# A list scheduler that plays the program through on another machine model: a two-layer diffusion block on one core

## Chip, cores and metric

The kernel runs on one core of one Trainium2 chip. The metric is device time in microseconds (us) of one execution; lower is better.

## What is computed

The reference is a two-layer block over 512 latent tokens and 256 context tokens of width 1024, batch 1, all in float32. Each layer normalises its input and shifts and scales it by vectors that come from a condition (adaptive modulation: six vectors of 1024 for each layer and each of the two streams). The first layer mixes tokens by pooling windows and a neighbourhood attention with context, the second by a recurrence over time (an RWKV layer) with heads of 64; each is followed by a squared-ReLU MLP. Two further layers with a gated MLP and a second mixer end the program. Cut to the parts that the change touches most:

```python
def rms_norm(x, g):
    y = xf * lax.rsqrt(jnp.mean(xf * xf, axis=-1, keepdims=True) + RMS_EPS)
    return (y * g.astype(jnp.float32)).astype(x.dtype)

def modulate(h, shift, scale):
    return h * (1 + scale) + shift

def neighbourhood_attention(q, k, v, k_ctx, v_ctx, rpb):
    ...
        s_lat = jnp.where(col_ok[:, None, :], s_lat + bias, NEG_INF)
        s_ctx = jnp.einsum('bqhd,bchd->bhqc', q_row, k_ctx).astype(jnp.float32) * scale
        s = jnp.concatenate([s_lat.reshape(B, NA_HEADS, GRID_W, kr * GRID_W), s_ctx], axis=-1)
        p = jax.nn.softmax(s, axis=-1).astype(v.dtype)
```

## The kernel before

The program is one launch of some 69,000 instructions. Matrices are multiplied in a three-term split: each float32 operand is held as a high and a low part (a cast on ScalarE writes `wh` from the loaded block `wr`, a subtraction on VectorE or GpSimd writes `wl`; activations have tiles `a` for both parts), and TensorE adds high*high, low*high and high*low. Weights are loaded on SyncE's one DMA queue in blocks of 512 KB through a ring of `wr` buffers.

The stages stand in this order in time. 0 to about 100 us: modulation for the first sub-layer, norms, keys and values of a memory. About 100 to 411 us: the first layer's mixer, that is its projections (`pj` banks), 24 units of attention (`ps` banks; VectorE adds the mask `nab` to the scores with a running maximum, ScalarE takes the exponent, VectorE splits and scales) and the pooled part (`pu`, `pw`, `t`), whose projection weights are `ev_u`. 411 to about 560 us: the tail of the pooled part, eight splits of the mixer's result (`a_874` to `a_881`), the output projection (`ev_o`), residual and norm. 600 to 1080 us: the first MLP. Then the recurrent layer's features to 1400 us, its recurrence (`wkv`) to 2120 us, its output and MLP to 2600 us, and the two last layers.

One job stands beside these. Each modulation vector block (128 outputs for one layer) needs a 512 KB block of `adaT` and two dot products on VectorE, one for each stream: `junk<-ada,c_rows` and `junk<-ada,cc_rows`, 128x1024 each, followed by a short read of the accumulator into `mod`. They will be called dots; there are 96 blocks, 192 dots. Blocks come through a ring of two buffers `ada` (the first 16 in part through `wr`), so the load of block m+2 waits on SyncE for the dots of block m. `First.ada_g` (line 552) writes the loop:

```python
for m in ms:
    w = c.ring(self.silp, [P, D], "ada", 2)
    nc.sync.dma_start(w, c.A["adaT"][i, m])
    yield from self.ada_dot(i, mod, m, [w], self.junk())
```

Blocks 0 to 15 of layer 0 are needed at the start; blocks 16 to 39 stand in the text beside the mixer; blocks 40 to 47 and the 48 of layer 1 (`ada` in `second_half`, line 1077, and `ada1`, line 1184) stand beside the output projection and the MLP that follows, and layer 1's are first used after that MLP, at about 1080 us.

What sets the order. The kernel's own planner (`Clock.weave`) decides in which order the Python text issues the instructions. The framework's `TileContext` then schedules this list: on a model of the machine, an engine that comes free takes, of its instructions whose operands the model has ready, the one that stands first in the list. So work that stands far behind may be put ahead into time that the model sees as free. Each engine then executes its instructions strictly in the order that results, and SyncE issues its DMAs in order, too.

## Time and profile before

| | before |
|---|---|
| time, median of 3 runs | 4526.43 us (4525.61 to 4526.72) |
| the profiled execution | 4529.56 us, of which 4527.8 us are the span from first to last instruction |
| TensorE (PE) busy | 4146.5 us, 92% of the span |
| VectorE (DVE) busy | 2583.0 us, 57% |
| ScalarE (ACT) busy | 1747.0 us, 39% |
| GpSimd (POOL) busy | 1150.1 us, 25% |
| mean granted TensorE clock | 0.945 of full speed |

All instructions are recorded by one helper, so they share the line L176; tiles and stretches of time tell them apart. The stages have different limits: TensorE is busy all the time in the MLPs, and in the mixers, the recurrence and the stretch around the output projection it has gaps. The profiled execution took 3.1 us more than the median of the runs.

### The profile page before, as it was taken

The page shows a single profiled execution, that of the slowest core. Times are in us where ns is not written, and L with a number is a line of the kernel's source. Part 1 is how long each engine was busy: PE and PEld are TensorE (multiplying, and loading weights), DVE is VectorE, ACT ScalarE, POOL GpSimd, SP SyncE. Part 2 cuts the span into 40 slices and gives each one's busy share as a digit, 9 for nine tenths or more (in the row PEclk, how much of TensorE's full clock was granted, in tenths as well). Part 3 has the DMA queues.
Part 4 walks back from the last instruction along what each step waited for, and adds up shares of the span by engine and source line. Part 5 has one row for each costly group of instructions (what it writes and reads, how often), then busy time and mean ns, then how long its engine had stood idle before and what let it go on. Part 6 is the DMA issues. An engine that isn't in the chain of part 4 may idle for free. (4 is left out here: it accounts for less than half of the span.)

```text
span 4527.8 us, 69045 instructions
## 1 busy us (share of the span) xinstructions
PE 4146.5 (92%) x27872; PEld 3436.0 (76%) x27872; DVE 2583.0 (57%) x4105; ACT 1747.0 (39%) x3265; POOL 1150.1 (25%) x1122
## 2 busy tenths in 40 slices
PE   5897899997897988887999999988999999979998
PEld 4786688886685777766888788876888888857887
DVE  8998844345934666677644543486433433584333
ACT  4454422223534556544522432225322322334222
POOL 4223300003514344453200211163201201353111
PEclk8898999999898899988999999998999999979999
DMA  6444421212233111112432322220332323211332
GB/s 220 148 134 134 148 75 62 65 63 96 84 122 102 42 46 52 47 40 63 137 107 94 98 95 97 93 76 18 103 98 94 97 96 96 93 38 62 97 98 84
DMA packets 193889, 408.80 MB, mean 90 GB/s; under 512 B 46496, under 2 KB 87456, under 8 KB 193568
## 3 DMA queue, kind: packets, MB, share of 16 engines
q1 hardware_dynamic: 193568, 404.37, 27.8%
q8 instruction: 219, 3.59, 0.3%
q14 instruction: 102, 0.84, 0.1%
HBM read 386.47 MB, written 17.83 MB: 89 GB/s over the span
## 5 line engine op out<-in xcount | busy, mean ns | idle before, releaser
L176 PE MATMUL pj<-a,wh 128*128 128x512 f32 (+1 forms) x5328 | 1420.2, 356 | 73.7 <-DVE a L176 32.2
L176 PE MATMUL ps<-a,wh 128*128 128x512 f32 x4192 | 1293.4, 390 | 12.0 <-DVE a L176 6.4
L176 ACT CAST wh<-wr 128x1024 fp32r<-128x1024 f32 (+3 forms) x548 | 565.2, 1031 | 1643.9 <-PE ps L176 952.6
L176 PEld LDWEIGHTS pj<-a,wh 128*128 128x128 f32 x5328 | 951.6, 195 | 221.8 <-issue 43.7
L176 PE MATMUL pj<-a,wl 128*128 128x512 f32 (+1 forms) x2664 | 939.2, 353 | 26.5 <-DVE wl L176 20.5
L176 PEld LDWEIGHTS ps<-a,wh 128*128 128x128 f32 x4192 | 786.5, 188 | 176.9 <-DVE a L176 7.5
L176 PE MATMUL ps<-a,wl 128*128 128x512 f32 x2096 | 815.5, 389 | 0.0
L176 DVE TENSOR_TENSOR wl<-wr,wh 128x1024 fp32r<-128x1024 f32 (+3 forms) x490 | 599.1, 1223 | 301.9 <-ACT wh L176 269.7
L176 PEld LDWEIGHTS pj<-a,wl 128*128 128x128 f32 x2664 | 517.9, 195 | 102.2 <-DVE wl L176 26.7
L176 PEld LDWEIGHTS ps<-a,wl 128*128 128x128 f32 x2096 | 393.8, 188 | 81.8
L176 POOL TENSOR_TENSOR t<-t,a 128x512 f32<-128x512 f32 x94 | 159.6, 1699 | 1113.4 <-ACT t L176 1113.4
L176 POOL TENSOR_TENSOR a<-a,t 128x512 f32<-128x512 f32 (+1 forms) x109 | 142.1, 1306 | 1023.0 <-ACT t L176 1021.6
L176 PE MATMUL ps<-a,a 128*128 128x256 f32 (+4 forms) x859 | 195.7, 383 | 35.4 <-ACT a L176 15.1
L176 ACT CAST f<-ps 128x512 f16<-128x512 f32 x312 | 178.0, 587 | 119.9 <-PE ps L176 117.9
L176 DVE SCALAR_TENSOR_TENSOR ytm<-ps,ytm 128x512 f32<-128x512 f32 x96 | 66.4, 692 | 264.9 <-PE ps L176 264.9
L176 DVE TENSOR_TENSOR t<-t,ps 128x512 f32<-128x512 f32 x87 | 59.8, 688 | 275.2 <-PE ps L176 270.6
L176 DVE TENSOR_TENSOR a<-a,pj 128x512 f32<-128x512 f32 (+1 forms) x176 | 101.2, 578 | 166.9 <-PE pj L176 166.9
L176 PEld LDWEIGHTS <-bd 128*128 128x128 f16 x3264 | 139.8, 102 | 72.3 <-issue 24.7
L176 PEld LDWEIGHTS ps<-a,a 128*128 128x128 f32 (+1 forms) x859 | 136.2, 212 | 73.0 <-ACT a L176 24.3
L176 POOL TENSOR_TENSOR wl<-wr,wh 128x1024 fp32r<-128x1024 f32 x58 | 150.8, 2605 | 148.1 <-ACT wh L176 126.2
L176 DVE TENSOR_TENSOR t<-ps,a 128x512 f32<-128x512 f32 x86 | 59.2, 691 | 220.5 <-PE ps L176 220.5
L176 DVE SCALAR_TENSOR_TENSOR a<-a,c_cvw,a 128x511 f32<-128x511 f32 (+15 forms) x180 | 177.7, 1007 | 2.3
(301 smaller groups left out, 5557.7 us busy)
## 6 DMA issues: line engine op xcount, KB each, us to landing
wr<-in_f1w SPq DMA_DIRECT2D x120, 512.0 KB, 3.5
wr<-in_f2w SPq DMA_DIRECT2D x120, 512.0 KB, 3.5
ada<-in_adaT SPq DMA_DIRECT2D x88, 512.0 KB, 3.6
wr<-in_m0w SPq DMA_DIRECT2D x76, 512.0 KB, 3.6
wr<-in_m1w SPq DMA_DIRECT2D x76, 512.0 KB, 3.6
wr<-in_ev_o SPq DMA_DIRECT2D x16, 512.0 KB, 3.9
wr<-in_w_o SPq DMA_DIRECT2D x16, 512.0 KB, 3.5
k<-d_k SPq DMA_DIRECT2D x48, 128.0 KB, 2.2
```

Source lines behind the costliest of these rows:

```text
L176: return real(*a, **k)
```

## The change

The scheduler is asked to play the program on its second machine model, a timeline simulator, in place of its default model. Nothing else in the kernel's text differs.

```diff
-    with tile.TileContext(nc) as tc:
+    with tile.TileContext(nc, schedule_with_timeline_sim=True) as tc:
         build(tc, A)
```

The instructions are the same ones (the same counts on every engine); their order on each engine differs in many places. Counted over the order of both kernels, with the dots that stand on VectorE ahead of one and the same instruction:

```
instruction on VectorE            its start before   dots ahead: before   after
first mask step near 148 us                  147.7                   55      67
a_385, near 200 us                           200.0                   76     100
sum4_495, near 250 us                        250.3                   93     130
rc_582, near 300 us                          300.5                  112     149
a_679, near 346 us                           346.0                  129     183
a_705, near 358 us                           358.5                  135     192
t_842 (pooled part), near 411 us             411.3                  151     192
ms_1036 (first norm), near 492 us            492.2                  180     192
```

**VectorE in the attention, shortly before 346 us.** `a_649` to `a_665` are splits of attention scores that TensorE multiplies next (`a<-ps,a`, 128x512); `junk_*` are the dots. Before:

```order
L176 ISA junk_1324_6052,mod_1220_5402<-ada_1323_6050,cc_rows_6_108,c_adab_72 128x1024
L176 ISA mod_1220_5402 128x1
L176 ISA junk_1326_6081,mod_1218_5400<-ada_1325_6079,c_rows_5_105,c_adab_72 128x1024
L176 ISA mod_1218_5400 128x1
L176 TENSOR_TENSOR a_654_2934<-ps_652_2928,a_653_2933 128x512
L176 TENSOR_TENSOR a_658_2943<-ps_656_2937,a_657_2942 128x512
L176 SCALAR_TENSOR_TENSOR t_715_3191<-pw_714_3189,pu_697_3146 128x512
L176 TENSOR_TENSOR a_662_2952<-ps_660_2946,a_661_2951 128x512
L176 TENSOR_TENSOR a_665_2974<-ps_663_2968,a_664_2973 128x512
L176 TENSOR_TENSOR a_668_2982<-ps_666_2976,a_667_2981 128x512
```

After, at the same splits:

```order
L176 ISA junk_1532_7350,mod_1218_5400<-ada_1531_7348,c_rows_5_105,c_adab_72 128x1024
L176 ISA mod_1218_5400 128x1
L176 ISA junk_1532_7350,mod_1220_5402<-ada_1531_7348,cc_rows_6_108,c_adab_72 128x1024
L176 ISA mod_1220_5402 128x1
L176 TENSOR_TENSOR a_654_2934<-ps_652_2928,a_653_2933 128x512
L176 TENSOR_TENSOR a_658_2943<-ps_656_2937,a_657_2942 128x512
L176 ISA junk_1545_7425,mod_1218_5400<-ada_1544_7423,c_rows_5_105,c_adab_72 128x1024
L176 ISA mod_1218_5400 128x1
L176 ISA junk_1545_7425,mod_1220_5402<-ada_1544_7423,cc_rows_6_108,c_adab_72 128x1024
L176 ISA mod_1220_5402 128x1
L176 TENSOR_TENSOR a_662_2952<-ps_660_2946,a_661_2951 128x512
L176 TENSOR_TENSOR a_665_2974<-ps_663_2968,a_664_2973 128x512
```

Before, two dots stand ahead of these splits and one step of the pooled part (`t_715`) among them; after, four dots (two whole blocks) stand ahead of and among them, and the blocks are later ones (`ada_1531` and `ada_1544` against `ada_1323` and `ada_1325`).

**VectorE at the splits ahead of the output projection, 427 to 438 us.** `a_878` to `a_881` and `a_874` on are the splits of the mixer's result, `wl_992` a split of an `ev_o` block. Before:

```order
L176 TENSOR_TENSOR a_878_3901<-a_200_708,a_870_3893 128x512
L176 ISA junk_1464_6914,mod_1218_5400<-ada_1463_6912,c_rows_5_105,c_adab_72 128x1024
L176 ISA mod_1218_5400 128x1
L176 TENSOR_TENSOR a_879_3902<-a_201_709,a_871_3894 128x512
L176 ISA junk_1464_6914,mod_1220_5402<-ada_1463_6912,cc_rows_6_108,c_adab_72 128x1024
L176 ISA mod_1220_5402 128x1
L176 TENSOR_TENSOR a_880_3903<-a_202_710,a_872_3895 128x512
L176 TENSOR_TENSOR wl_992_4071<-wr_990_4068,wh_991_4070 128x1024
L176 TENSOR_TENSOR a_881_3904<-a_203_711,a_873_3896 128x512
L176 ISA junk_1473_6981,mod_1218_5400<-ada_1472_6979,c_rows_5_105,c_adab_72 128x1024
L176 ISA mod_1218_5400 128x1
```

After:

```order
L176 TENSOR_TENSOR a_878_3901<-a_200_708,a_870_3893 128x512
L176 TENSOR_TENSOR a_879_3902<-a_201_709,a_871_3894 128x512
L176 TENSOR_TENSOR wl_992_4071<-wr_990_4068,wh_991_4070 128x1024
L176 TENSOR_TENSOR a_880_3903<-a_202_710,a_872_3895 128x512
L176 TENSOR_TENSOR a_881_3904<-a_203_711,a_873_3896 128x512
L176 TENSOR_TENSOR a_874_3897<-a_196_704,a_866_3889 128x512
L176 TENSOR_TENSOR a_875_3898<-a_197_705,a_867_3890 128x512
L176 TENSOR_TENSOR a_876_3899<-a_198_706,a_868_3891 128x512
L176 TENSOR_TENSOR a_877_3900<-a_199_707,a_869_3892 128x512
```

All dots are gone from between the splits: none is left at this point.

**TensorE in the attention, at 341 to 350 us.** `ps_*` are attention products; `pj_719` and `pj_789` are the projections of the pooled part (`ev_u`), of the first and the second of its four groups. Before:

```order
L176 MATMUL ps_688_3096<-a_584_2619,a_637_2871 128x512
L176 MATMUL ps_688_3096<-a_585_2620,a_637_2871 128x512
L176 MATMUL ps_688_3096<-a_584_2619,a_638_2872 128x512
L176 MATMUL ps_690_3102<-a_583_2618,a_637_2871 128x256 x2
L176 MATMUL ps_690_3102<-a_583_2618,a_638_2872 128x256
L176 MATMUL ps_690_3102<-a_583_2618,a_637_2871 128x256 x2
L176 MATMUL ps_690_3102<-a_583_2618,a_638_2872 128x256
L176 MATMUL pj_719_3198<-a_151_563,wl_641_2880 128x512
L176 MATMUL pj_719_3198<-a_152_564,wh_640_2879 128x512
L176 MATMUL pj_719_3198<-a_160_572,wh_640_2879 128x512
```

After, at a place of the attention that comes earlier (`ps_663` was at about 340 us):

```order
L176 MATMUL ps_663_2968<-c_ident_61,a_618_2775 128x128 x4
L176 MATMUL ps_646_2895<-a_653_2933,a_405_1694 128x256
L176 MATMUL pj_789_3510<-a_170_582,wh_717_3194 128x256
L176 MATMUL pj_789_3510<-a_166_578,wl_718_3195 128x256
L176 MATMUL pj_789_3510<-a_167_579,wh_717_3194 128x256
L176 MATMUL pj_789_3510<-a_171_583,wh_717_3194 128x256
L176 MATMUL pj_789_3510<-a_167_579,wl_718_3195 128x256
L176 MATMUL pj_789_3510<-a_167_579,wh_717_3194 128x256
L176 MATMUL pj_789_3510<-a_171_583,wh_717_3194 128x256
L176 MATMUL pj_789_3510<-a_167_579,wl_718_3195 128x256
```

Before, most of the first group's projection (`pj_719`) stands behind the products of the unit with `ps_690`; after, the second group's (`pj_789`) already stands among products ahead of them. Over the whole order, 91 rows `pj<-a,wh` and `pj<-a,wl` that stood behind `ps_678` (the input of `a_679`) stand ahead of it now; with the durations that they had in the trace of before these are 16.8 us of TensorE.

On SyncE, in the same stretch, the last `adaT` load (`ada_7707`) stood 50 loads behind the first load of `ev_o` (`wr_4062`) and now stands five ahead of it. At the start, two mask loads (`nab`, 458 KB each) now stand ahead of `adaT` loads that were ahead of them. From 600 to 1040 us every engine has the order it had. In the later stages instructions change places with their neighbours; the work ahead of one and the same instruction differs by mostly under 5 us in either direction (at a few places of the features and the last mixers by up to 20 us) and comes back to zero within each stage.

## Rows read from the trace of the kernel before

**Rows 1.** The page's head and part 1: span, busy time of each engine.

```profile
span 4527.8 us, 69045 instructions
...
PE 4146.5 (92%) x27872; PEld 3436.0 (76%) x27872; DVE 2583.0 (57%) x4105; ACT 1747.0 (39%) x3265; POOL 1150.1 (25%) x1122
```

**Rows 2.** Busy time by stretch (us), TensorE's clock, share of DMA, GB/s.

```profile
core 0: us, PE busy (x) PEld busy (x) DVE busy (x) ACT busy (x) POOL busy (x), PEclk, DMA share, GB/s
0.00:100.00 100.00, 55.52 (x203) 36.08 (x204) 85.71 (x122) 46.96 (x105) 43.50 (x35) 0.88 0.65 227
100.00:346.00 246.00, 217.70 (x1331) 192.10 (x1330) 225.61 (x478) 122.04 (x302) 59.48 (x28) 0.90 0.42 141
346.00:411.00 65.00, 57.26 (x342) 50.06 (x341) 56.62 (x144) 40.55 (x100) 20.14 (x20) 0.92 0.32 105
411.00:427.00 16.00, 4.15 (x8) 1.86 (x7) 13.31 (x29) 4.82 (x10) 8.77 (x9) 0.58 0.46 144
427.00:444.00 17.00, 7.50 (x18) 5.32 (x18) 17.00 (x22) 7.38 (x17) 10.93 (x8) 0.50 0.45 144
444.00:560.00 116.00, 101.94 (x504) 81.06 (x503) 96.00 (x126) 49.69 (x84) 42.47 (x30) 0.93 0.53 170
...
600.00:1000.00 400.00, 400.00 (x2292) 352.66 (x2291) 162.20 (x239) 96.06 (x144) 0.00 (x0) 1.00 0.20 63
```

**Rows 3.** The same stretches, the dots alone (instructions that read `ada`).

```profile
100.00:346.00 246.00, 142.94 (x95) 0.90 0.42 141
346.00:411.00 65.00, 31.84 (x23) 0.92 0.32 105
411.00:427.00 16.00, 7.17 (x6) 0.58 0.46 144
427.00:444.00 17.00, 9.05 (x6) 0.50 0.45 144
444.00:560.00 116.00, 45.05 (x30) 0.93 0.53 170
```

**Rows 4.** VectorE's groups by form, 100 to 411 us: the dots.

```profile
L176 DVE CUSTOM_DVE_ANT_0 junk<-ada,cc_rows,c_adab 128x1024 bf16<-128x1024 f32 x58 | 92.2, 1590 | 0.6
L176 DVE CUSTOM_DVE_ANT_0 junk<-ada,c_rows,c_adab 128x1024 bf16<-128x1024 f32 x59 | 83.0, 1408 | 10.0 <-DMA ada<-in_adaT 9.5
```

**Rows 5.** What VectorE waited for, 100 to 346 us: total us, times, longest.

```profile
DVE junk L176 <- DMA ada<-in_adaT: 7.8, 8, 1.8
DVE a L176 <- ACT a L176: 4.8, 6, 1.4
```

**Rows 6.** VectorE in order of time, 427 to 438 us: start, duration.

```profile
427.66 1.75 DVE L176 CUSTOM_DVE_ANT_0 junk<-ada,c_rows,c_adab 128x1024 bf16<-128x1024 f32 x1
...
429.34 1.20 DVE L176 TENSOR_TENSOR a<-a,a 128x512 fp32r<-128x512 f32 x1
430.47 1.27 DVE L176 CUSTOM_DVE_ANT_0 junk<-ada,cc_rows,c_adab 128x1024 bf16<-128x1024 f32 x1
...
434.47 1.21 DVE L176 TENSOR_TENSOR a<-a,a 128x512 fp32r<-128x512 f32 x1
435.60 1.74 DVE L176 CUSTOM_DVE_ANT_0 junk<-ada,c_rows,c_adab 128x1024 bf16<-128x1024 f32 x1
...
437.27 1.20 DVE L176 TENSOR_TENSOR a<-a,a 128x512 fp32r<-128x512 f32 x1
```

**Rows 7.** TensorE in order of time, ahead of the output projection; idle before in brackets.

```profile
432.18 1.22 PE L176 MATMUL pj<-a,wh 128*128 128x512 f32 x2 [4.19 <-ACT a L176]
438.53 0.79 PE L176 MATMUL pj<-a,wh 128*128 128x512 f32 x1 [5.13 <-DVE a L176]
```

**Rows 8.** Busy time by stretch: features, recurrence, one late mixer; columns as in 2.

```profile
1040.00:1400.00 360.00, 308.40 (x1566) 251.83 (x1564) 207.39 (x302) 149.44 (x263) 134.32 (x154) 0.92 0.31 101
1400.00:2120.00 720.00, 614.33 (x10410) 501.02 (x10410) 488.48 (x942) 401.41 (x919) 315.05 (x452) 0.89 0.17 48
2960.00:3130.00 170.00, 142.56 (x662) 110.64 (x660) 134.31 (x255) 60.67 (x157) 82.35 (x68) 0.86 0.14 46
```

## The prediction

> **What bounds the kernel now.** The page's first part comes first: TensorE is busy 92% of the span, VectorE 57% [rows 1]. That average hides that the stages have different limits, so the next view is busy time by stretch [rows 2]. In the first MLP (600 to 1000 us) TensorE is busy 400.00 of 400 us and VectorE 162.20: nothing there waits for VectorE, and a delay that comes into this stretch goes through it unreduced. In the first mixer it is the other way round. From 100 to 346 us VectorE is busy 225.61 of 246 us (92%), TensorE 217.70 (88%); from 346 to 411 us the two have 56.62 and 57.26 of 65 us. The third view, the dots alone in the same stretches [rows 3], shows what fills VectorE: 142.94 us of the 225.61 are dots, of which none feeds the attention. The attention's own steps need 82.7 us there. Behind the mixer, 444 to 560 us, VectorE is busy 96.00 of 116 us, 45.05 of it dots.
>
> So the stretch from 100 to 411 us is set by VectorE and TensorE together, with little slack in either, and whatever is put into VectorE's queue there in front of the attention's steps makes these later.
>
> **The change, part by part.** The instructions are the same; only places change. I price each move with durations of the trace.
>
> *Dots moved ahead of the attention.* By the counts in the section on the change, 129 dots stand ahead of `a_679` (346 us) before, 183 after: 54 more. Later, at 358 us, all 192 are ahead. The dots that now run from 346 us on take 31.84 + 7.17 + 9.05 + 45.05 = 93.11 us in 65 entries [rows 3] (63 dots, two of them across a boundary), 1.43 us each; those of 100 to 411 us take 1.41 and 1.59 us, by the two forms [rows 4]. 54 x 1.43 = 77.3 us of VectorE are put in front of `a_679`.
>
> How much of this hides? VectorE's idle time up to there is 246 - 225.61 = 20.4 us [rows 2]. If the added dots squeeze out all of it, `a_679` is 77.3 - 20.4 = 56.9 us late; if none, 77.3 us. Of the idle time 7.8 us are dots that waited for their own load [rows 5]: with more dots in a row this part doesn't shrink. I take the other 12.6 us as squeezed out: 64.7 us late. The rest of the idle time is steps that waited for ScalarE and TensorE [rows 5], which will be ahead of VectorE then.
>
> *From there to the end of the mixer.* VectorE has less left than before: of 56.62 us in 346 to 411 us the dots' 31.84 go, and the last 9 dots (192 - 183) come, 12.9 us: 37.7 us. TensorE has 57.26 us less the 16.8 us of pooled projections that its order now puts ahead of that point: 40.5 us. The larger, TensorE, sets this part: 40.5 us back to back, or 46.0 us at the 88% that it reached before. Against the 65 us of before this gives back 24.5 or 19.0 us. The mixer's end is late by 56.9 - 24.5 = 32.4 us at the least, 77.3 - 19.0 = 58.3 us at the most while the 16.8 us are really done in the holes that the late attention leaves, and 64.7 - 19.0 = 45.7 us as I take it. If TensorE can't do the projections ahead (their weights stand behind `adaT` loads on SyncE, which wait for dots), it is 77.3 us.
>
> *Dots that are gone behind the mixer.* At 427 to 438 us three dots of 1.75, 1.27 and 1.74 us stand in turn between splits of the mixer's result [rows 6]; the last of the splits shown ends at 438.47, and TensorE starts its next product at 438.53 after 5.13 us idle [rows 7]. Without them the split comes some 4.5 us sooner (their durations less the overlap of some 0.1 us): -4.5. In 411 to 427 us 7.17 us of dots stand in a chain of short steps while TensorE does only 4.15 us of work in 16 [rows 2, 3]; some stood in waits, so I take half, -3.6, between 0 and -7.2. From 444 to 560 us TensorE is idle 14.1 us in all and 45.05 us of dots leave; I take -3, between 0 and -14.1. Sum -11, from -4.5 to -25.8.
>
> *The start.* Two mask loads of 458 KB each go ahead of `adaT` loads. At the 227 GB/s of that stretch [rows 2] they take 4.0 us, and VectorE, at 85.71 of 100 us, needs those dots. I take half, +2, between 0 and +8 (the same again for a store that now stands among them).
>
> *The later stages.* From 600 to 1040 us the order is the same: 0, TensorE being full. In the features, the recurrence and the late mixers TensorE has 51.6, 105.7 and 27.4 us of idle time in the stretches shown [rows 8], but moves there are small and of both signs, and no engine has more work ahead of it at a stage's end: 0, within 15 either way.
>
> *Sum*, against the profiled execution (4527.8 us of span and 1.8 around it, 4529.6): 45.7 - 11 + 2 + 0 = +36.7, so 4566.3. That execution was 3.1 us above the median of the runs; taken off, **4563 us**.
>
> A rule of the Trainium skill gives another result. Its page "Perfetto Trace Analysis" (section "Identifying the Most-Contended Engine") names the engine with the highest occupancy as the one that matters; for TensorE it goes by the weight loads' busy share. Over the whole kernel that is TensorE by either measure (92%, or 76% of weight loads, against 57%), so moving VectorE's work would be free: the first rival below. The page's next section adds that the most contended engine can change from regime to regime and that such regimes may be interleaved; by that sentence work should leave this mixer for the MLP, the opposite of what the change does.
>
> **The rivals.**
>
> *The dots hide.* TensorE is the kernel's bound, its order has changed as well, and the late attention is filled with projections; what is late at 411 us is caught up by 560, where 61.3 us of dots have left VectorE [rows 3]. For it: TensorE is 88% busy in this stretch, nearly as busy as VectorE. Against it: the catch-up is bounded by TensorE's idle time from 411 to 560 us, 11.9 + 9.5 + 14.1 = 35.4 us [rows 2], and even all of that only meets the smallest delay, 32.4. It would give 4526, within 9.
>
> *The changed order is faster elsewhere.* The place is the recurrence and the features, with 105.7 and 51.6 us of TensorE idle, and the late mixers (27.4 us in the one shown) [rows 8]; the mechanism is that a step which TensorE waits for is put ahead of one that nobody waits for. It decides when it saves more than 36.7 + 9 = 46 us. A third of the 184.7 us, 61.6, would give 4563 - 62 = 4501. For it: these stages are bound by chains across engines, where order matters. Against: the moves there are mostly under 5 us.
>
> *No overlap at all.* The dots' loads and the weights queue up on SyncE, the projections stay where they are, and 77.3 us arrive at the end: 77.3 - 4.5 + 8 = +81, 4607.
>
> *That the change does nothing* is excluded: the order differs on every engine.
>
> **How the numbers follow.** What counts as no change is 0.2%, 9 us: about what a measurement of this kernel can tell. My forecast, the mixer late by 32 to 58 us with its give-backs: 0.68. No overlap: 0.08. Hidden: 0.11. Faster elsewhere: 0.13. So slower 0.76, same 0.11, faster 0.13. The forecast's own range is 32.4 - 25.8 - 5 = +2 to 58.3 - 4.5 + 8 + 10 = +72 on 4526, that is 4528 to 4598. The range for 8 in 10 reaches from the lower edge of the hidden case, 4517, to 4598; it leaves out the faster case and most of the one without overlap.
>
> **What would show it.** In the profile after, VectorE should be busy over 95% from 100 us on until the last dot, near 420 us, and no dot should run after about 430; the splits ahead of the output projection should stand back to back, with the 5.13 us gap of [rows 7] gone or short; the first MLP's stretch of a fully busy TensorE should begin some 35 us later; TensorE's idle time should grow by 50 us or so up to 400 us. If VectorE is idle by 10% there, the dots wait for loads and the delay is at its upper end. If the MLP begins as early as before, the dots were hidden. If it begins 35 us late and the whole is not slower, the later stages gave it back, and the shift between the two traces will say which.

## The result, and the profile after

The changed kernel is slower: 4584.88 us, median of 4 runs (4581.53 to 4589.25), against 4526.58 us before; the ratio is 1.0129 (95% interval 1.0112 to 1.0147). The forecast was 4563 with 4517 to 4598. The profiled execution took 4587.51 us, its span is 4585.7.

The page's head and part 1 of the changed kernel:

```profile
span 4585.7 us, 68997 instructions
...
PE 4170.1 (91%) x27872; PEld 3456.7 (75%) x27872; DVE 2564.0 (56%) x4105; ACT 1747.5 (38%) x3265; POOL 1138.3 (25%) x1122
```

Against [rows 1] the span is 57.9 us longer. TensorE does the same 27872 matmuls and is busy 23.6 us longer (4170.1 - 4146.5); the other 34.3 us are idle time. A lower granted clock doesn't account for the 23.6 us: the mean over the span is 0.942 of full speed against 0.945, but over TensorE's busy time alone it is 0.957 and 0.956. What does account for them is not shown.

Both programs have the same number of matmuls, so the start of the n-th one in each trace can be compared. The table (worked out from the traces) has the delay against the kernel before, in us, at the matmul that started at about the time in the head row there; the other rows are the experiments. Inside the mixer the n-th matmul of two orders need not be the same product, so a step of VectorE can be later there than the table says.

```
us in the kernel before                  110    150    250    300    350    437    590   1000   2300   4490
changed kernel                           9.9   14.0   40.4   36.6   60.2   60.4   48.0   46.8   55.2   56.1
e1  last 40 dots late                   11.0   15.8   40.5   36.6   50.6   36.6   50.4   49.3   61.5   60.8
e3  all 112 late                        10.3   14.6   18.8    5.6    8.6   -4.7  -12.3  -13.4    1.8   -2.8
e4  before, all 112 late                -0.9   -3.0   -5.8  -16.5  -19.3  -34.3  -45.0  -29.5  -28.9  -36.2
e6  start's splits on VectorE            0.4    5.4   29.8   24.7   46.0   48.9   45.7   44.5   65.1   60.4
e7  dots paced as before                10.0   14.0   29.8   16.7   32.9   44.9   49.3   48.2   58.9   54.5
e8  before, paced in the same way       -0.2   -2.0   -1.8   -1.8   -0.1   -2.6   -4.6   -4.6   -4.4   -5.6
e5  before, dots through the MLP         0.1    0.4   -3.6  -14.3  -17.1  -32.1  -40.9  -41.0  -42.9  -50.6
e9  dots through the MLP                11.0   15.2   19.5    6.3    9.3   -4.0  -11.6  -12.8    4.7    0.4
e10 VectorE in before's order           -0.6   -1.0    6.2    1.3   16.2   32.2   45.6   44.5   50.3   44.2
e11 before, VectorE in after's order    25.2   33.2   58.9   59.7   90.2   97.0   95.6   95.2   96.6   92.2
e12 TensorE in before's order           11.3   16.4   45.0   46.8   64.0   59.5   48.9   47.7   54.6   53.3
e13 VectorE, ScalarE in before's order   0.5    0.4   14.0    8.7   24.7   41.4   57.5   56.3   69.7   71.2
```

So the delay of the changed kernel grows in the start (9.9) and in the mixer (60.4 at 437 us, at the projection's product behind the gap of [rows 7]), 12.4 us come back from there to 590 us, and the MLP changes it by 1.2. The recurrent layer adds 8 (46.8 to 55.2).

Busy time by stretch of the changed kernel, cut at the same instructions as [rows 2] (`a_679` now starts at 423.4 us, the splits at 492, the first MLP's full stretch near 648):

```profile
109.00:423.40 314.40, 246.42 (x1414) 210.33 (x1413) 294.74 (x591) 125.07 (x300) 62.16 (x34) 0.86 0.46 152
423.40:476.00 52.60, 36.11 (x194) 30.55 (x193) 33.27 (x101) 32.98 (x83) 8.16 (x14) 0.77 0.10 32
497.00:608.00 111.00, 103.29 (x523) 83.14 (x523) 52.78 (x65) 51.27 (x84) 39.60 (x34) 0.95 0.36 118
648.00:1047.00 399.00, 399.00 (x2293) 352.46 (x2292) 162.74 (x239) 95.99 (x144) 0.00 (x0) 1.00 0.20 64
```

The second and third columns of figures are TensorE and its weight loads, the fourth is VectorE. In the first row VectorE is busy 294.74 of 314.40 us (93.7%, where over 95% was forecast): idle 19.7, where the 246 us of before had 20.4 [rows 2]. The dots alone in the same stretches:

```profile
109.00:423.40 314.40, 203.09 (x144) 0.86 0.46 152
423.40:476.00 52.60, 11.20 (x9) 0.77 0.10 32
476.00:497.00 21.00, 0.00 (x0) 0.76 0.26 81
```

As the order said, no dot is left behind the mixer. What VectorE waited for from 109 to 423.4 us (total us, times, longest):

```profile
DVE junk L176 <- DMA ada<-in_adaT: 14.9, 16, 1.8
DVE a L176 <- PE ps L176: 2.3, 2, 1.6
DVE a L176 <- POOL hr L176: 0.5, 1, 0.5
DVE a L176 <- ACT a L176: 0.3, 1, 0.3
```

Waits for other engines went as expected (ScalarE 4.8 to 0.3, [rows 5]); the dots' waits for their own loads nearly doubled, 7.8 to 14.9 us, and used up what was saved. The splits ahead of the output projection, VectorE in order of time, and TensorE's gaps there (idle before in brackets):

```profile
492.00 0.69 DVE L176 TENSOR_TENSOR a<-a,a 128x512 fp32r<-128x512 f32 x1
493.13 0.69 DVE L176 TENSOR_TENSOR a<-a,a 128x512 fp32r<-128x512 f32 x1 [0.44 <-ACT a L176]
494.07 1.41 DVE L176 TENSOR_TENSOR wl<-wr,wh 128x1024 fp32r<-128x1024 f32 x1 [0.26 <-ACT wh L176]
495.41 5.76 DVE L176 TENSOR_TENSOR a<-a,a 128x512 fp32r<-128x512 f32 x5
```

```profile
496.62 1.22 PE L176 MATMUL pj<-a,wh 128*128 128x512 f32 x2 [3.87 <-ACT a L176]
498.95 0.80 PE L176 MATMUL pj<-a,wh 128*128 128x512 f32 x1 [1.10 <-DVE a L176]
```

The gap of 5.13 us in [rows 7] is 1.10 now: that step of the prediction holds. The first product of the projection is 64.4 us late (432.18 to 496.62), the one behind the gap 60.4.

### The profile page after: what moved, and what is told of

The parts are those of the page before. It is cut to its first block, busy times and chain, and to the rows that moved or that the text cites. A ratio compares the mean times of both kernels' runs of the same rounds, so it can differ in the third digit from the quotient of the medians.

```text
span 4585.7 us, 68997 instructions
## 1 busy us (share of the span) xinstructions
PE 4170.1 (91%) x27872; PEld 3456.7 (75%) x27872; DVE 2564.0 (56%) x4105; ACT 1747.5 (38%) x3265; POOL 1138.3 (25%) x1122
## 5 line engine op out<-in xcount | busy, mean ns | idle before, releaser
L176 PE MATMUL ps<-a,a 128*128 128x256 f32 (+4 forms) x859 | 190.3, 374 | 34.5 <-ACT a L176 16.5
L176 PEld LDWEIGHTS ps<-a,a 128*128 128x128 f32 (+1 forms) x859 | 128.9, 204 | 70.2 <-ACT a L176 25.8
L176 DVE SCALAR_TENSOR_TENSOR a<-a,c_cvw,a 128x511 f32<-128x511 f32 (+17 forms) x180 | 166.6, 950 | 1.3
```

The lines of the kernel that those rows point to most:

```text
L176: return real(*a, **k)
```

## Experiments

In e1, e3 to e5 and e7 to e9 dots are held back by their bias: a small VectorE step writes a copy of it that depends on another tile, and later dots read the copy.

```diff
+    def gate(self, by):
+        t = self.pool.tile(list(self.adab.shape), F32, name="c_adab2")
+        for i in range(2):
+            self.c.nc.vector.scalar_tensor_tensor(t[:, i], by[:, :48], 0.0, self.adab[:, i], op0=ALU.mult, op1=ALU.add)
+        return t
```

**e1, the changed kernel, the last 40 dots behind the mixer.**

```diff
+        self.late = self.gate(yh[0][1][3].bitcast(F32))
...
-        yield from self.ada_g(1, tiles_mod(tiles), range(48))
+        yield from self.ada_g(1, tiles_mod(tiles), range(28))
+        self.adab = self.late
+        yield from self.ada_g(1, tiles_mod(tiles), range(28, 48))
```

> The changed kernel with the dots of the last 20 blocks made to wait for the splits behind the mixer (one small VectorE step hands them their bias); by the order 152 dots then stand ahead of the end of the attention instead of 192 (139 before the change), but 140 still stand ahead of its middle, as in the changed kernel. If dots ahead of the attention make it late: at the step near 346 us 31 dots fewer than in the changed kernel, 31 x 1.43 = 44 us of its 77 us delay are gone; the first MLP starts 15 to 25 us later than before instead of 48; total 4540 to 4560. If the delay comes from the other moves (start, TensorE, loads): total stays at 4575 to 4590.

Measured 4594.33 us, ratio 1.0147 (1.0132 to 1.0162). The delay at 437 us falls from 60.4 to 36.6, so the dots did hold up the end of the attention. But by 590 us it is back at 50.4: the same dots now stand between the splits and the first norm, and this stretch loses 13.8 us where the changed kernel gains 12.4 in it, 26 us of difference. Neither case of the expectation had said that, and the time lies above both: moved from the mixer's end to behind it, 40 dots gain nothing.

**e3 and e4, both kernels, all 112 later dots behind the first norm.** The same edit in both (e4 in the kernel before):

```diff
                 yield ("h", i, KD - 1)
+            self.adab = self.gate(h[1][1][KD - 1].bitcast(F32))
             yield from self.ada_g(0, tiles_mod(mtiles), range(40, 48))
```

> The changed kernel with all 112 dots that the text places beside the MLP made to wait for the first norm behind the mixer (near 580 us); 80 dots then stand ahead of the whole attention. If dots ahead of the attention make it late: 103 dots fewer ahead of the step near 346 us than in the changed kernel, more than its whole delay; VectorE is no longer the limit there and TensorE's idle time of 100 to 560 us shrinks below that of before. The 112 dots take 160 us of the 238 us that VectorE is idle in the first MLP: hidden, its length grows by under 3 us. Total 4490 to 4520. If the MLP pays for the dots' loads (512 KB each on the same queue as its weights): its stretch grows by 10 us or more. If the other moves set the delay: 4560 to 4590.

> The kernel before with the same 112 dots made to wait in the same way, so the default model's order with 80 dots ahead of the attention instead of 107 to 139. If VectorE's dots hold up the mixer before the change too: 49 dots fewer ahead of the step near 346 us (70 us of VectorE), TensorE's 36 us of idle time from 100 to 411 us and 35 us from 411 to 560 us shrink by a half: total 4485 to 4510, and below the run of the changed kernel with the same edit by what the other moves cost (start and later stages, 10 to 20 us). If TensorE is the limit of the mixer already: 4520 to 4530.

Measured 4526.84 us, 0.9997 (0.9988 to 1.0006), and 4496.22 us, 0.9929 (0.9914 to 0.9943). e3 lies between the cases of its expectation, e4 in its first. The dots cost both orders a good deal: 60 us at 1000 us in the changed kernel (46.8 to -13.4), 29.5 in the other. But with 80 dots ahead of the attention in each, the two still differ by 33 us at 590 us. There are costs of the new order in which the moved dots have no part.

**e6, the changed kernel, the start's splits moved from GpSimd to VectorE.**

```diff
-                c.split(w[0][a], w[1][a], self.wm[l * 4 + q][h], g)
+                c.split(w[0][a], w[1][a], self.wm[l * 4 + q][h], v)
```

> The changed kernel with the 16 splits of the memory's weights at the start (128x512) moved from GpSimd to VectorE. In the changed kernel the first 32 dots take 53.7 us, 46.4 before, and end 11 us later; slow dots (over 1.3 us) occur only beside GpSimd work. If GpSimd's work beside them makes the dots longer: the first 32 dots fall to 41 to 45 us, the splits add 11 us to VectorE, and the first norm's gains come within 5 us of the changed kernel's 82.6 us. If the later dots came from later loads: the dots keep their 53 us or wait for loads, and the gains come 10 us later still, at 92.

Measured 4589.0 us, 1.0129 (1.0112 to 1.0146). The first 32 dots, from 0 to the first norm's gains, in the changed kernel (to 82.56 us) and in e6 (to 76.20 us):

```profile
0.00:82.56 82.56, 53.74 (x32) 0.91 0.72 251
```

```profile
0.00:76.20 76.20, 42.87 (x32) 0.94 0.79 275
```

With GpSimd busy 13.25 us there in place of 43.69, the dots take 42.87 us, and the gains come 6.4 us sooner in spite of 16 more VectorE steps. The start's delay is gone (0.4 at 110 us), 11 us are still ahead at 437, but only 2 at 590: in between the granted clock of TensorE was 0.87 to 0.93 from 560 to 640 us, in the changed kernel 0.91 to 1.00. Whether the lower clock or the waits beside it cost the 9 us is not shown. The start is a real loss of the changed order, but mending it alone doesn't shorten the whole.

**e7 and e8, both kernels, the 112 dots released in four steps** as the attention of each quarter of the tokens ends, so that both have nearly the dots of the kernel before ahead of each step:

```diff
+        self.late = [self.gate(y[0][4 + t]) for t in range(4)]
         yh = [c.slots_hl(8), c.halves_hl(8)]
...
         for m in ms:
+            b = i * 48 + m - 40
+            if b >= 0:
+                self.adab = self.late[(b >= 9) + (b >= 24) + (b >= 35)]
```

> The changed kernel with the 112 later dots released in four steps, each when the attention of one quarter of the tokens is done, so that its order has nearly as many dots ahead of each step as the kernel before (102, 131, 147 and 154 of 192 where the kernel before has 107, 129, 139 and 154 and the changed kernel 141, 184, 192 and 192). All other moves of the change stay. If the dots' places are the whole cause beside the start: only the start's 10 us are left at the first MLP instead of 48, and with the 8 us of the later stages the total is 4540 to 4550. If the other moves in the mixer cost by themselves what the two kernels without these dots differ by (33 us at the start of the first MLP, 30 in the total): 4555 to 4565. If the dots' places are nothing: 4580 to 4590.

> The kernel before with the same four steps; its order hardly changes (107, 129, 138 and 153 dots ahead). This prices the steps themselves: 4520 to 4532, no difference, by every theory; if it is slower by more than 10 us, the runs with such steps are to be read against this one.

Measured: e7 4581.72 us, 1.0120 (1.0103 to 1.0138); e8 4523.75 us, 0.9989 (0.9977 to 1.0000). The steps themselves cost nothing, and with the dots back in their places the changed kernel is 3 us faster by the medians, inside its runs' spread. In the table e7 is 15.5 us ahead of the changed kernel at 437 us (44.9 against 60.4) and 1.3 behind at 590. That is the third case of its expectation: in the sum the dots' places are nothing. Two differences are left. 12 dots more than in e8 stand ahead of the first mask step (67 against 55), among blocks that the steps don't hold, and 4 more ahead of `a_385` (80 against 76). And the scheduler plans anew with the edit, so some other instructions of e7 change places against the changed kernel as well.

**e5 and e9, both kernels, the 112 dots spread through the first MLP**, eight blocks after each of its parts:

```diff
+            self.adab = self.gate(h[1][1][KD - 1].bitcast(F32))
+            self.pace = Y2[0][KD - 1]
...
+            if b > 0 and b % 8 == 0:
+                yield ("ch", b // 8 - 1)
+                self.adab = self.gate(self.pace)
...
+            c.clock.signal(("ch", ch))
             if ch == 7:
                 done(group[0])
```

> The kernel before with the 112 dots released in seven steps through the first MLP instead of all at its start. The run with all at once gained 45 us up to the MLP and gave 15 back in its first 200 us, where VectorE was 90% busy. If the crowd of dots at the MLP's start was the reason: the 15 us come back, total 4478 to 4488. If the dots' loads on the weights' queue were the reason: the loss is only spread, total 4490 to 4500.

> The changed kernel with the same seven steps. Its run with all dots at once lost under 1 us in the MLP, so 4520 to 4528 if the steps matter only where VectorE's queue was crowded; the difference to the kernel before with the same edit is then 35 to 45 us and is what the other moves cost in the start, the mixer and the later stages. If it comes within 15 us of that kernel, the other moves cost little and the difference of 30 us in the earlier pair came from somewhere else.

Measured: e5 4479.63 us, 0.9896 (0.9879 to 0.9912); e9 4528.13 us, 1.0001 (0.9991 to 1.0010). e5 beats both kernels. The first 200 us of its MLP against those of e4 (columns as in [rows 2]):

```profile
546.70:746.70 200.00, 199.98 (x1147) 176.46 (x1148) 152.88 (x254) 46.43 (x70) 0.00 (x0) 1.00 0.45 145
```

```profile
546.70:746.70 200.00, 193.82 (x1089) 170.12 (x1090) 185.09 (x307) 41.67 (x64) 0.00 (x0) 0.98 0.56 183
```

With VectorE at 152.88 in place of 185.09 us TensorE has no gap, and the time is in the range that the expectation gave for the crowd as the reason; but its loads are thinner as well (145 against 183 GB/s). And the crowd alone doesn't do it: e3 has as many dots at its MLP's start, VectorE is busy 95% there, and TensorE is full:

```profile
590.00:790.00 200.00, 200.00 (x1151) 176.77 (x1151) 189.08 (x317) 47.98 (x72) 0.00 (x0) 1.00 0.57 187
```

So crowd and loads cost time there in the order of before and none in the order of the changed kernel, which gains nothing by spreading them (e3 4526.84, e9 4528.13). What sets the two orders apart there was not looked for. The pair e5, e9 differs by 29 us at 590 us (-11.6 against -40.9) and by 48.5 us in the end; most of that growth comes in the recurrent layer (28.2 at 1000 us, 47.6 at 2300).

**e10, e11, e12, e13: one or two engines held to the other kernel's order** up to 600 us, by order edges between the instructions as they stand there, with no instruction added:

```diff
+ORDERS = [
...
+def impose(nc, tc, order):
+    have = {i.name: i for i in nc.cur_bb.bb.instructions}
...
+            if prev is not None:
+                tc.add_manual_dep(i, prev.name, mybir.DependencyInfo(mybir.DependencyClass.NoSync, mybir.DependencyReason.DATA), reason="order")
...
         build(tc, A)
+        impose(nc, tc, ORDERS)
```

> The changed kernel with VectorE alone held to the order of the kernel before up to 600 us (order edges, no added instruction), dots included: 107, 129, 139 and 154 dots ahead as before; the other engines are scheduled on the timeline model around it. If VectorE's order, dots and steps together, carries the delay: the first MLP starts within 12 us of before, total 4530 to 4545 (the 8 us of the later stages stay). If the orders of TensorE, ScalarE or SyncE carry it, as the run with the paced dots suggests: 4565 to 4590.

> The kernel before with VectorE alone held to the order of the changed kernel up to the same point, so 141, 184, 192 and 192 dots ahead; the others are scheduled on the default model around it. If VectorE's order carries the delay: the first MLP 40 to 50 us later than before, total 4565 to 4580. If other engines' orders carry it: 4525 to 4545.

> The changed kernel with TensorE alone held to the order of the kernel before up to 600 us; VectorE's dots stay early (146, 183, 192). If TensorE's order (projections ahead of attention products) carries the delay: 4530 to 4550. If VectorE's does, by dots or steps: 4570 to 4590, and without the projections to fill the holes perhaps 10 us more.

> The changed kernel with VectorE and ScalarE both held to the order of the kernel before up to 600 us; TensorE, GpSimd and SyncE stay with the timeline model. With VectorE alone held, the delay was gone up to 300 us and came back as 32 us by the mixer's end and 46 us by the first MLP, with TensorE waiting 43 us for ScalarE's results in 60 to 480 us where it waited 16 before. If ScalarE's order carries this second part: the first MLP starts within 12 us of before, total 4530 to 4542. If the orders of TensorE or SyncE carry it: 4560 to 4580.

Measured: e10 4572.67 us, 1.0102 (1.0084 to 1.0120); e11 4623.07 us, 1.0217 (1.0202 to 1.0233); e12 4586.0 us, 1.0136 (1.0120 to 1.0152); e13 4594.51 us, 1.0148 (1.0131 to 1.0165). With VectorE's old order the delay is gone up to 300 us (1.3 against 36.6), then it grows to 32 at 437 and 46 at 590. The old order of TensorE alone changes nothing (48.9 at 590). The other two lie above both cases of their expectations. e11 is slower than either parent, by 38 us than the changed kernel, and 25 us of its delay are there at 110 us already; e13 is 10 us above the changed kernel, with intervals that overlap. So a mixture of orders brings waits of its own, and what one of these runs gains or loses can't be put down to the engine that was held alone. Who TensorE waited for from 60 to 480 us, first in the changed kernel, then in e10:

```profile
PE ps L176 <- ACT a L176: 45.9, 23, 9.3
PE pj L176 <- ACT a L176: 26.2, 1, 26.2
PE pj L176 <- DVE a L176: 22.0, 10, 4.2
```

```profile
PE ps L176 <- ACT a L176: 43.4, 26, 7.6
PE pj L176 <- DVE a L176: 15.7, 6, 6.2
```

In the kernel before, the same view gives 15.9 us in 10 waits for the first of these. The attention's products wait 27 to 30 us more for ScalarE's results in both runs, with VectorE's dots early or in their old places. e13 says that ScalarE's own order is not what makes it late there (its sum is 42.0). Nor is ScalarE where the wait begins, up to 300 us: it waits itself for `nb`, VectorE's step behind the running maximum. In the changed kernel (109 to 337 us), and in the kernel before (100 to 300 us):

```profile
ACT a L176 <- DVE nb L176: 36.9, 6, 11.3
```

```profile
ACT a L176 <- DVE nb L176: 20.1, 4, 10.6
```

In the like stretch it is 31.7 us in e7, with the dots back, and 15.2 in e10, with VectorE in the old order. From there to the mixer's end this wait is as before (6.8 against 6.1), while the products still wait 25.7 us for ScalarE against 6.9.

## Why the prediction was right, and where it was not

**The number and the sign** were right, and so was most of what the trace was to show. The reason given for them was not the whole reason, and by the experiments not even the larger part. That the sum came out in the range owes something to luck: the start, the mixer and the later stages cost more than was set down, and the stretch behind the mixer gave back more.

*Dots moved ahead of the attention.* `a_679` is 77.4 us late (346.0 to 423.4). That is the upper end of the step, 77.3, only by chance: 9.9 us of it are the start's, a term of its own, so 67.5 us are left against the 64.7 that were taken. How they came about is another matter. The price of a dot was misread: the 93.11 us are those of 63 dots, 1.48 us each and not 1.43 (in the changed kernel a dot of this stretch took 1.41). And some of the 54 dots run before 109 us already, and from there on the dots take 60.2 us more than before (203.09 against 142.94), VectorE's other steps 9.0 us more. The "other 12.6 us as squeezed out" failed: the dots' own load waits rose by 7.1 us, and VectorE's idle time stayed at 19.7.

*From there to the end of the mixer.* VectorE's 33.27 and TensorE's 36.11 busy us in 52.6 us are below the 37.7 and 40.5 of the step; the stretch took 52.6 where 46.0 was taken, because neither engine was the limit: TensorE was idle 16.5 us. So the mixer's end, the 411 us of before, is 65.0 us late (77.4 less the 12.4 that the shorter stretch gives back), or 55.1 without the start, where 45.7 was taken and 58.3 was the bound.

*Dots that are gone behind the mixer.* From 65.0 to 48.0, 17 us came back against 11, inside the step's -4.5 to -25.8: 0.6 up to the projection's first product (-3.6 was taken), 4.0 at the gap (-4.5) and 12.4 behind it (-3). This is the step that misled all the same, together with the first. Taken as a price of the dots' places it is too small: e7 puts them back, wins 15.5 us up to 437 us and loses 16.8 behind it (+4.4 in place of -12.4). Moving these dots from behind the mixer to ahead of its end costs nothing in sum. The 35 us that the forecast set down to them belong, by e7, to the two steps below.

*The start.* 9.9 us at 110 us (11.1 at the first gains) against 2. The loads that I had priced are not it. Of VectorE's time up to the gains the 32 dots take 53.74 us instead of 46.35; e6 shows that GpSimd's work beside them makes the difference, since GpSimd is busy 43.69 us there in place of 28.14. The rest is other steps of VectorE, among them four short memory steps (2.9 us) that stood behind the gains before; its idle time up to the gains did not grow (14.25 us before, 13.73 after).

*The mixer's other moves* were no term at all; I had only credited the 16.8 us of projections put ahead. Between 150 and 590 us they cost 38 us with dots in like places (e7 less e8: 53.9 at 590, 16.0 at 150) and 14 without the dots (e9 less e5: 29.3 less 14.8). What this is made of is settled in part: up to 300 us it goes with VectorE's order (e10), whose `nb` steps come later and hold up ScalarE, and behind that TensorE waits for ScalarE's results. TensorE's order alone doesn't mend it (e12), nor those of VectorE and ScalarE together (e13). That the projections put ahead leave TensorE nothing to do while the last units' exponents are computed fits these waits, but is only argued; VectorE and TensorE held together would have told, and weren't tried.

*The later stages* cost 8 us, within the 15 allowed. The first MLP began 48 us late, not some 35.

The rivals: that the dots hide failed at 437 us (60.4 late). That the order is faster elsewhere failed: no stage after 590 us gave back more than the MLP's 1.2 us. The Trainium skill's rule of the most contended engine ("Perfetto Trace Analysis", section "Identifying the Most-Contended Engine") would have moving dots cost nothing. The trace disagrees at the mixer's end, and so do e3 and e9, which gain 58 and 57 us on the changed kernel by an edit that moves dots; that e7 gains nothing agrees with the rule in the sum alone. What the same page of the Trainium skill says of interleaving regimes (section "Optimization Strategy") is borne out by e5: 112 dots taken out of the mixer and the stretch behind it into the MLP, where VectorE was busy 41% before, gave 1.04%.

## What to carry to other kernels

When a schedule changes as a whole, the most visible move need not be the one that costs: price it by putting only that move back, in both orders, before believing it. Here filler work cost the same in the mixer and in the stretch right behind it, where VectorE was busy 92% and 83% before (e7 against the changed kernel); it paid to move it into a stretch where VectorE was busy 41% (e3, e4, e5 and e9), and in one of the two orders to spread it there (e5 16.6 us below e4, e9 no better than e3). An order taken for one engine from another schedule may be slower than both schedules (e11).

## What was not expected of the hardware

A dot (128x1024, float32 inputs) takes 1.26 to 1.29 us in all 141 cases of the changed kernel in which no GpSimd instruction ran beside it. In the other 51 it took up to 3.47 us, 1.94 in the mean. In order of time, VectorE and then GpSimd in the changed kernel:

```profile
38.31 1.28 DVE L176 CUSTOM_DVE_ANT_0 junk<-ada,cc_rows,c_adab 128x1024 bf16<-128x1024 f32 x1
39.64 2.96 DVE L176 CUSTOM_DVE_ANT_0 junk<-wr,c_rows,c_adab 128x1024 bf16<-128x1024 f32 x1
```

```profile
37.10 1.74 POOL L176 TENSOR_TENSOR mem_rs<-mem_rs,mhalf 128x2 f32<-128x2 f32 x1 [4.82 <-DMA a<-in_ctx]
38.81 2.71 POOL L176 TENSOR_TENSOR nab<-nab,c_namask 128x896 f32<-128x896 f32 x1
```

Which of the two began first decides. The dot at 38.31 began ahead of the GpSimd step at 38.81 and took its usual time. The dot at 39.64 began while that step ran, and ends 1.1 us after it, which is about a dot's own time: it looks as if it stood still beside it. All 51 cases fit. The 17 dots that began first took at most 1.29 us. The 26 long ones began with a GpSimd step running (one together with it), and each ended 1.08 to 1.09 us after that step's end. The 8 that took their usual time all the same began beside a step of two or four columns or one with at most 0.1 us left. GpSimd's steps waited as well: the `nab` step shown took 2.71 us, and the shortest of its form 2.08. The Trainium skill, "Trainium Architecture — The Big Picture", section "What this means for kernel authors", says that VectorE and GpSimd share a port pair under an exclusive lock; these cases agree.
